# Slopes folded into Q, small work moved off GpSimd, and tables recorded beside the MLPs in a three-block transformer kernel

## The chip, the cores and the metric

One core of a Trainium2 chip runs the whole program. The metric is the device time of one execution in microseconds (us). TensorE, VectorE (DVE in the rows), ScalarE (ACT), GpSimd (POOL) and SyncE (SP, which issues the DMAs) each run their own instructions in order and wait for each other by semaphores.

## The reference, cut to what matters

The input is one sequence of 512 tokens with 1024 features, in float32. Block 1 is an MLA attention (12 heads, rotary part of 32) with a cross attention on 256 memory rows, then an MLP with squared ReLU. Block 2 has a sliding-window attention (SWA, 12 query heads over 4 key heads, ALiBi slopes and sinks) and again cross attention and MLP. Block 3 has a gated short convolution beside an NSA attention (compressed, selected and windowed keys, 8 heads, rotary part of 64), a gated merge, and an FFN with a width-3 causal convolution.

```python
# SWA: scores, slopes, sinks
sc = jnp.einsum('bnqhgd,bnkhd->bnhgqk', q, kk) * (HEAD_DIM ** -0.5)
dist = (pos_q[..., :, None] - pos_k[..., None, :]).astype(jnp.float32)
sc = sc - slopes[None, None, :, :, None, None] * dist[:, :, None, None]
sc = jnp.where(valid[None, :, None, None], sc, NEG)
p = jax.nn.softmax(jnp.concatenate([sc, sink], axis=-1), axis=-1)[..., :-1]
# second block: rotation by positions_2, y_a = a_b * conv(a_c * a_x)
# FFN: g = causal_dwconv(gu[..., :D_FF_2], w) + b; x + (silu(g) * gu[..., D_FF_2:]) @ w_ffn_out
```

## The kernel before

Everything is kept transposed: features on the 128 partitions, the 512 tokens along the free axis, so that the state is eight tiles `x` of 128x512. Float32 products are made of rounded parts: each weight chunk of 128x512 is loaded (`raw`), rounded by ScalarE (`h`), and the rest is taken by a subtraction (`l`); activations are split in the same way. `dense` then does three matmuls for each block of 128 features: h by h, h by l, l by h, into a PSUM bank (`psd`), and an eviction function follows. `fetch_chunk` does the loading and splitting: the subtraction lies on GpSimd for the chunks whose first key begins with one of `POOL_KEYS` (SWA's Q, the convolution path, MLA's uq and ukv), otherwise on VectorE.

`Norm.tile` squares each feature tile on ScalarE and adds the squares up, on GpSimd unless the caller says VectorE; `Boundary.tile` does so for two norms at once. `normalize` divides softmax rows on GpSimd; `rope` and `proj_group` rotate by a product with `cos` on GpSimd and one with `sin` on VectorE; `conv` makes the first of three taps on GpSimd. In SWA, `scores` makes for each head a bias of the distance table `nd` times eight times the slope, on GpSimd, which the masking instruction in `soft` adds to the scores. `rope_tables` makes sine and cosine of 512 positions with 11 instructions on VectorE and two Sin activations on ScalarE.

The program is first recorded (`Trace.add`, with the instructions that each depends on) and then ordered by a planner, `Trace.schedule`. It simulates the five engines with the costs of `_op_cost`. Whenever an engine is free, it takes the ready instruction of the highest priority, which is the recording order (`later` shifts it). An instruction whose page or PSUM bank can't be had yet is parked (the test below); an instruction of a much later part may start early if it is ready and the pages claimed up to its own part leave room for its page. What this gives is the order in which each engine runs the program. Weight loads are shifted forward by 80 instructions.

```python
            for t in o.tiles:
                if t.slot is None:
                    k = t.key
                    if not free[k] or (t.first > cur and load[k][cur:t.first].max() >= cap[k]):
                        return k
```

Tiles: `pgf` and `pgr` are the page pools (20 of float32, 50 of rounded float32), `sm` small columns, `psd`, `pss`, `pst`, `pso` PSUM banks (dense, scores, transposes, outputs), `cstt` the constants, `vecs` the gains. All recorded instructions have one line, L414, so rows are told apart by tiles.

Of the kernel before, what the change touches and what calls it, by code (L numbers as in the profile page):

```python
# [11 lines left out]
FT = mybir.dt.float32  # L12
# [5 lines left out]
P = 128  # L18
# [9 lines left out]
AHEAD = 80  # L28
POOL_KEYS = ("swa_q", "n_a", "uq", "ukv")
NFR = 50  # L30
# [151 lines left out]

NCST = 648


def pack_const():
    c = np.zeros((P, NCST), np.float32)
    i = np.arange(P)
    c[i, i] = 1.0
    c[i ^ 16, 128 + i] = 1.0  # L190
    c[:, 256:384] = np.where(i[None, :] <= i[:, None], 0.0, BIG)
    rel = 128 + i[:, None] - np.arange(256)[None, :]
    c[:, 384:640] = np.where((rel >= 0) & (rel < 128), 0.0, BIG)
    inv32 = (10000.0 ** (-(np.arange(16) * 2.0) / 32)).astype(np.float32)
    inv64 = (10000.0 ** (-np.arange(32) / 32.0)).astype(np.float32)
# [5 lines left out]
    c[:, 645] = i >= 64  # L201
    return c

# [146 lines left out]
class Trace:  # L350
    def __init__(self, nc):
        self.real_nc = nc
        self.ops = []
        self.bias = 0
        for name in ENGINES:
            setattr(self, name, Recorder(self, name))

    @contextmanager
    def later(self, n):
        self.bias += n  # L360
        yield
        self.bias -= n

    def add(self, name, method, args, kw):
# [31 lines left out]
        for v in writes:  # L396
            t, b = v.tile, v.box()
            t.writes = [w for w in t.writes if not (b[0] <= w[1][0] and b[1] >= w[1][1] and b[2] <= w[1][2] and b[3] >= w[1][3])]
            t.reads = [w for w in t.reads if w[0] == o.i or not (b[0] <= w[1][0] and b[1] >= w[1][1] and b[2] <= w[1][2] and b[3] >= w[1][3])]
            t.writes.append((o.i, b))  # L400
        o.preds = preds
        out_costs = writes if writes else [v for v in reads]
# [132 lines left out]
class Norm:  # L535
    def __init__(self, net, src, gains, d, name, into=None, adder="gpsimd"):
        self.into, self.adder = into, getattr(net.nc, adder)
        self.net, self.src, self.gains, self.d, self.name = net, src, gains, d, name
        self.n = src[0].shape[-1]
        self.h = [None] * len(src)  # L540
        self.l = [None] * len(src)
        self.acc = None
# [24 lines left out]
class Boundary:  # L567
# [9 lines left out]
    def tile(self, m):  # L577
# [3 lines left out]
        for j in range(2):  # L581
# [4 lines left out]
            else:  # L586
                q = net.pg("bq")
                nc.scalar.activation(q, x, AF.Square, **kw)
                nc.gpsimd.tensor_tensor(self.acc[j], self.acc[j], q, op=OP.add)

# [22 lines left out]
class Net:  # L613
    def __init__(self, ctx, tc, aps):
# [9 lines left out]
        self.wtiles = {}  # L624
        self.first_key = {}
        for key, j, _, _ in self.plan:
            self.first_key.setdefault(self.blocks[key, j][0], key)

# [24 lines left out]
    def fetch_chunk(self, i):  # L653
# [7 lines left out]
        nc.scalar.copy(h[:, :n], raw[:, :n])  # L661
        eng = nc.gpsimd if self.pool_chunk(i) else nc.vector
        eng.tensor_tensor(l[:, :n], raw[:, :n], h[:, :n].bitcast(FT), op=OP.subtract)
        self.wtiles[i] = (h, l)

    def pool_chunk(self, i):
        return self.first_key[i].startswith(POOL_KEYS)

# [302 lines left out]
    def mla(self, nx, osh, osl):  # L971
# [67 lines left out]
        def proj_group(g):  # L1039
            def rev(p):  # L1040
# [4 lines left out]
                nc.vector.tensor_tensor(w, r, sin, op=OP.mult)  # L1045
                nc.gpsimd.tensor_tensor(u, u, cos, op=OP.mult)
                nc.vector.tensor_tensor(u, u, w, op=OP.add)
# [8 lines left out]
        def proj_pair(p):  # L1056
# [8 lines left out]
            def kev(ps):  # L1065
                for j in range(2):
                    h = 2 * p + j
                    K[h] = self.pg("K")
                    nc.scalar.copy(K[h][0:64], ps[64 * j:64 * j + 64])
                    nc.gpsimd.tensor_scalar(K[h][64:96], kr[64:96], 1.0, 1.0, op0=OP.mult, op1=OP.mult)  # L1070
            self.dense([(f"uq_n{p}", P, qev)], ch[:3], cl[:3])
# [27 lines left out]
        for p in range(6):  # L1099
# [8 lines left out]
            os_set(p, out)  # L1108

    def swa(self, nx, osh, osl):  # L1110
        nc = self.nc
# [45 lines left out]
        nc.vector.tensor_scalar(nsink, self.vec("sinks", 0, 12), -1.0, None, op0=OP.mult)  # L1157

# [8 lines left out]
        def proj_pair(p):  # L1167
            def ev(ps):
                u = self.pg("sq")
                nc.vector.tensor_tensor(u, ps, nx.R, op=OP.mult)  # L1170
                Q[2 * p], Q[2 * p + 1] = self.qstack(u, "sqs")
            self.dense([(f"swa_q{p}", P, ev)], nx.h, nx.l)

        def scores(h):
            k1, k2 = kk[h // 3]
            slope8 = 8.0 * float(np.float32(2.0 ** (-8.0 * (h + 1.0) / 12.0)))
            bias = [self.pg("sb") for _ in range(2)]
            B = [bias[b // 2][:, (b % 2) * 256:(b % 2) * 256 + 256] for b in range(4)]
            nc.gpsimd.tensor_scalar(bias[0][:, 128:], nd[0][:, 128:], slope8, 1.0, op0=OP.mult, op1=OP.mult)
            nc.gpsimd.tensor_scalar(bias[1], nd[1], slope8, 1.0, op0=OP.mult, op1=OP.mult)  # L1180
            nm, sm = self.sm("nm"), self.sm("sum")
# [3 lines left out]
            for b in range(4):  # L1185
# [4 lines left out]
                self.mm(p[:, :n], Q[h][:, b * P:b * P + P], k2[:, k0:k0 + n], False, True)  # L1190
                self.soft(p[:, :n], n, B[b][:, 256 - n:], 0.125, nsink[:, h:h + 1], nm[:, b:b + 1], sm[:, b:b + 1], dst[b])
            e = self.sm("se")
# [37 lines left out]

    def mlp(self, i, nx, after):
        nc = self.nc
# [17 lines left out]
        first = True  # L1250
        for kind, b in MLP_ORDER:
            if kind == "up":
# [7 lines left out]
    def first_block(self, stop):  # L1260
        for i in range(2):
# [9 lines left out]
            if i == 0:  # L1271
                self.mlp(i, n2, nx.tile)
                nx.finish()
            elif stop == "mlp1":
                self.mlp(i, n2, lambda m: None)
            else:
                b = Boundary(self)
                self.mlp(i, n2, b.tile)
                b.finish()
                return b  # L1280
            if stop == f"mlp{i}":
                return

    def second_block(self, nx, stop):
# [12 lines left out]
        nc.sync.dma_start(sel, self.a["sel"])  # L1297
        posr = self.pg("posr2", I32)
        pr = self.a["posr2"]
        nc.sync.dma_start(posr, bass.AP(tensor=pr.tensor, offset=pr.offset, ap=[[0, P], [1, S]]))  # L1300
        cos, sin = self.rope_tables(posr, self.cst[:, 642:643], self.cst[:, 643:644], "r64")
        blk2 = self.cst[:, 644:646]
# [185 lines left out]
        def a_path(m):  # L1488
# [218 lines left out]
```

## Time and profile before

| | |
|---|---|
| runs shown, median (lowest, highest) | 1887.12 us (1885.49, 1887.37) |
| profiled execution, its own time | 1889.12 us |
| its span in the profile | 1887.3 us |
| TensorE matmul busy | 1848.9 us, 98% |
| VectorE busy | 1163.5 us, 62% |
| ScalarE busy | 836.9 us, 44% |
| GpSimd busy | 354.3 us, 19% |
| mean granted clock of TensorE | 0.995 |

The span reaches from the first to the last instruction of the profiled execution, whose own time lies a little outside it. The stages, by the slices of the page: MLA and cross attention to 215 us, output product and first MLP to 600, SWA to 737, output product and second MLP to 1098, the boundary and NSA to 1350, the merge to 1530, the FFN to the end.

### The profile page before, as it was taken

How to read it: one execution, taken by the hardware profiler on the slowest of the kernel's cores; microseconds unless marked ns; L12 is line 12 of the kernel's file. 1: busy time of each engine (PE TensorE's matmuls, PEld its weight loads, DVE VectorE, ACT ScalarE, POOL GpSimd, SP SyncE). 2: the span in 40 equal slices, each digit the busy share in tenths (PEclk: the TensorE clock that was granted, in tenths of full speed). 3: DMA queues.
4: the chain of work that ended last, by engine and by line, in shares of the span. 5: the costliest groups of instructions: out<-in, count | busy, mean ns of one | idle time of the engine just before them, and what ended most of it. 6: DMA issues, size and time to landing. Idle time of an engine off the chain costs nothing.

```text
span 1887.3 us, 25092 instructions
## 1 busy us (share of the span) xinstructions
PE 1848.9 (98%) x8749; PEld 1522.6 (81%) x8749; DVE 1163.5 (62%) x2293; ACT 836.9 (44%) x1674; POOL 354.3 (19%) x406
## 2 busy tenths in 40 slices
PE   7999999999999998999999999999999999999998
PEld 6877788888888876888888887778888888888887
DVE  8977954444546688544434367777755567774752
ACT  7688544242324676442324245457533333332321
POOL 1263300000001553000000041555200122110100
PEclk9999999999999999999999999899999999999999
DMA  5412233333333221333333323211133333333332
GB/s 188 125 42 61 67 102 99 95 98 98 95 95 90 69 56 45 98 98 96 98 98 95 98 63 101 76 51 40 58 99 98 98 89 99 98 98 97 95 100 72
DMA packets 92151, 166.99 MB, mean 88 GB/s; under 512 B 10612, under 2 KB 12408, under 8 KB 92024
## 3 DMA queue, kind: packets, MB, share of 16 engines
q1 hardware_dynamic: 92024, 165.40, 30.3%
q8 instruction: 68, 1.11, 0.2%
q14 instruction: 59, 0.48, 0.1%
HBM read 161.68 MB, written 2.10 MB: 87 GB/s over the span
## 4 chain that ended last, share of the span: by engine, by line
PE 89%; DVE 7%; ACT 2%; issue 1%; DMA 1%; POOL 0%; SPq 0%; DVEq 0%; ACTq 0%; POOLq 0%
PE psd L414 79%; PE pst L414 4%; PE pss L414 3%; DVE pgf L414 3%; PE pso L414 3%; DVE pgr L414 2%; DVE l L414 1%; DVE sm L414 1%; ACT pgf L414 1%; ACT pgr L414 0%; DMA raw<-w 0%; DVE x L414 0%; POOL pgf L414 0%; SPq L414 0%; ACT h L414 0%
## 5 line engine op out<-in xcount | busy, mean ns | idle before, releaser
L414 PE MATMUL psd<-pgr,h 128*128 128x512 f32 (+1 forms) x4590 | 1435.2, 392 | 13.1 <-ACT pgr L414 12.0
L414 PEld LDWEIGHTS psd<-pgr,h 128*128 128x128 f32 x4590 | 858.7, 188 | 191.5 <-ACT pgr L414 13.1
L414 PE MATMUL psd<-pgr,l 128*128 128x512 f32 (+1 forms) x2295 | 897.0, 391 | 0.0
L414 DVE TENSOR_TENSOR l<-raw,h 128x512 fp32r<-128x512 f32 (+1 forms) x551 | 430.1, 783 | 457.1 <-ACT h L414 455.0
L414 ACT CAST h<-raw 128x512 fp32r<-128x512 f32 (+2 forms) x601 | 369.2, 616 | 696.9 <-PE psd L414 602.5
L414 PEld LDWEIGHTS psd<-pgr,l 128*128 128x128 f32 x2295 | 432.3, 188 | 88.3 <-issue 1.9
L414 POOL TENSOR_TENSOR pgf<-pgf,pgf 128x512 f32<-128x512 f32 (+1 forms) x96 | 128.5, 1342 | 1058.4 <-ACT pgf L414 769.9
L414 DVE TENSOR_TENSOR pgr<-pgf,pgr 128x512 fp32r<-128x512 f32 (+4 forms) x184 | 127.4, 694 | 12.5 <-ACT pgr L414 7.4
L414 ACT CAST pgr<-pgf 128x512 fp32r<-128x512 f32 (+4 forms) x184 | 108.2, 590 | 54.0 <-POOL pgf L414 31.0
L414 ACT ACTIVATE pgf<-pgf 128x512 f32<-128x512 f32 (+2 forms) x125 | 74.8, 602 | 110.6 <-DVE pgf L414 110.5
L414 DVE TENSOR_TENSOR pgf<-psd,pgf 128x512 f32<-128x512 f32 (+2 forms) x100 | 65.5, 657 | 57.5 <-PE psd L414 55.9
L414 PE MATMUL pso<-pgr,pgr 128*128 128x512 f32 (+3 forms) x368 | 90.0, 340 | 5.3 <-DVE pgf L414 2.9
L414 DVE TENSOR_TENSOR pgr<-pst,pgr 128x512 fp32r<-128x512 f32 (+1 forms) x126 | 73.8, 610 | 14.3 <-ACT pgr L414 14.1
L414 POOL TENSOR_TENSOR l<-raw,h 128x512 fp32r<-128x512 f32 (+1 forms) x50 | 67.4, 1357 | 75.4 <-ACT h L414 43.7
L414 POOL TENSOR_SCALAR pgf<-pgf,sm 128x256 f32<-128x256 f32 (+3 forms) x128 | 69.2, 558 | 62.7 <-DVE sm L414 46.3
L414 PE MATMUL pst<-cstt,pgf 128*128 128x128 f32 x436 | 75.4, 277 | 2.5 <-POOL pgf L414 1.1
L414 DVE CUSTOM_DVE_ANT_0 pgf<-pss,cmask 128x256 f32<-128x256 f32 (+3 forms) x144 | 65.4, 470 | 17.6 <-PE pss L414 16.2
L414 ACT CAST pgr<-pst 128x512 fp32r<-128x512 f32 (+1 forms) x126 | 62.8, 529 | 27.0 <-PE pst L414 25.9
L414 PEld LDWEIGHTS pso<-pgr,pgr 128*128 128x128 f32 x368 | 58.4, 189 | 19.6 <-ACT pgr L414 7.2
L414 PE MATMUL pss<-pgr,pgr 128*128 128x256 f32 (+4 forms) x320 | 68.6, 309 | 3.9 <-DVE sm L414 3.5
L414 ACT ACTIVATE pgf<-pgf,sm 128x256 f32<-128x256 f32 (+3 forms) x128 | 65.8, 516 | 14.1 <-DVE sm L414 13.7
L414 PEld LDWEIGHTS pst<-cstt,pgf 128*128 128x128 f32 x436 | 52.1, 140 | 19.2 <-POOL pgf L414 6.3
(119 smaller groups left out, 1137.0 us busy)
## 6 DMA issues: line engine op xcount, KB each, us to landing
raw<-w SPq DMA_DIRECT2D x588, 256.0 KB, 2.6
x<-xT SPq DMA_DIRECT2D x8, 256.0 KB, 5.5
out<-x SPq DMA_DIRECT2D x8, 256.0 KB, 2.0
pgf<-pgf SPq DMA_DIRECT2D x24, 64.0 KB, 2.0
pgf<-aux SPq DMA_DIRECT2D x5, 256.0 KB, 2.7
pgf<-memT SPq DMA_DIRECT2D x4, 256.0 KB, 5.4
raw<-w SPq DMA_DIRECT2D x7, 140.0 KB, 2.1
raw<-w SPq DMA_DIRECT2D x4, 192.0 KB, 2.7
```

The source lines that it names most:

```text
L414: getattr(getattr(nc, names[o.eng]), o.method)(*[r(x) for x in o.args], **{k: r(v) for k, v in o.kw.items()})
```

## The change

`POOL_KEYS` goes: all weight splits are on VectorE. The norm and boundary adds, the rotary products with `cos`, the copies of the rotary key into `K`, and the two page products of the convolution path move from GpSimd to VectorE. The first tap of `conv` moves from GpSimd to ScalarE. GpSimd keeps `normalize`, NSA's gating, the merge sum and the FFN's gate product. In SWA, Q is divided by eight times the slope when it is evicted (six new constant columns), the distance table is added as it stands, and the scale in `soft` becomes 0.125 times that number; the 24 bias instructions go. The distance tables of SWA and the 64-wide rotation tables of the second block are recorded in the first and the second MLP, after its first two steps; for the latter the position load (`hold`) depends on the last instruction recorded before it.

```diff
+    @contextmanager
+    def hold(self):
+        self.held = len(self.ops) - 1
+        yield
+        self.held = None
...
+        if self.held is not None:
+            preds.add(self.held)
...
-    def __init__(self, net, src, gains, d, name, into=None, adder="gpsimd"):
+    def __init__(self, net, src, gains, d, name, into=None, adder="vector"):
...
-                nc.gpsimd.tensor_tensor(self.acc[j], self.acc[j], q, op=OP.add)
+                nc.vector.tensor_tensor(self.acc[j], self.acc[j], q, op=OP.add)
...
-        eng = nc.gpsimd if self.pool_chunk(i) else nc.vector
-        eng.tensor_tensor(l[:, :n], raw[:, :n], h[:, :n].bitcast(FT), op=OP.subtract)
+        nc.vector.tensor_tensor(l[:, :n], raw[:, :n], h[:, :n].bitcast(FT), op=OP.subtract)
...
-                nc.gpsimd.tensor_tensor(u, u, cos, op=OP.mult)
+                nc.vector.tensor_tensor(u, u, cos, op=OP.mult)
...
-                    nc.gpsimd.tensor_scalar(K[h][64:96], kr[64:96], 1.0, 1.0, op0=OP.mult, op1=OP.mult)
+                    nc.vector.tensor_copy(K[h][64:96], kr[64:96])
...
+    def swa_positions(self):
...
+        self.swa_tables = ND, nsink
...
-                nc.vector.tensor_tensor(u, ps, nx.R, op=OP.mult)
+                nc.vector.scalar_tensor_tensor(u, ps, self.cst[:, 646 + p:647 + p], nx.R, op0=OP.mult, op1=OP.mult)
...
-            nc.gpsimd.tensor_scalar(bias[0][:, 128:], nd[0][:, 128:], slope8, 1.0, op0=OP.mult, op1=OP.mult)
-            nc.gpsimd.tensor_scalar(bias[1], nd[1], slope8, 1.0, op0=OP.mult, op1=OP.mult)
...
-                self.soft(p[:, :n], n, B[b][:, 256 - n:], 0.125, nsink[:, h:h + 1], nm[:, b:b + 1], sm[:, b:b + 1], dst[b])
+                self.soft(p[:, :n], n, ND[b][:, 256 - n:], float(0.125 * SLOPE8[h]), nsink[:, h:h + 1], nm[:, b:b + 1], sm[:, b:b + 1], dst[b])
...
-        for kind, b in MLP_ORDER:
+        for step, (kind, b) in enumerate(MLP_ORDER):
+            if step == 2:
+                aside()
...
+    def nsa_tables(self):
+        nc = self.nc
+        posr = self.pg("posr2", I32)
+        pr = self.a["posr2"]
+        with nc.hold():
+            nc.sync.dma_start(posr, bass.AP(tensor=pr.tensor, offset=pr.offset, ap=[[0, P], [1, S]]))
+        self.rope64 = self.rope_tables(posr, self.cst[:, 642:643], self.cst[:, 643:644], "r64")
...
-            nc.gpsimd.tensor_tensor(u, u, cos, op=OP.mult)
+            v.tensor_tensor(u, u, cos, op=OP.mult)
...
-                nc.gpsimd.tensor_tensor(t, t, nx.R, op=OP.mult)
+                v.tensor_tensor(t, t, nx.R, op=OP.mult)
...
-                nc.gpsimd.tensor_tensor(u, u, st["y"], op=OP.mult)
+                v.tensor_tensor(u, u, st["y"], op=OP.mult)
...
-            nc.gpsimd.tensor_scalar(y, t, w[2], 1.0, op0=OP.mult, op1=OP.mult)
+            nc.scalar.activation(y, t, AF.Copy, scale=w[2])
...
-            nc.gpsimd.tensor_scalar(y, t, w[2], b, op0=OP.mult, op1=OP.add)
+            nc.scalar.activation(y, t, AF.Identity, scale=w[2], bias=b)
```

## Rows read from the trace of the kernel before

**Rows 1.** Table by stage: length, busy time (instructions) of each engine, granted clock, DMA.

```profile
50.00:200.00 150.00, 148.23 (x841) 118.99 (x842) 124.32 (x354) 118.71 (x288) 62.31 (x86) 1.00 0.26 73
...
640.00:705.00 65.00, 62.76 (x351) 50.18 (x349) 55.30 (x144) 49.86 (x135) 34.60 (x55) 1.00 0.18 50
705.00:737.00 32.00, 25.20 (x156) 20.39 (x155) 28.34 (x80) 24.93 (x68) 13.72 (x26) 1.00 0.07 17
737.00:1098.00 361.00, 361.00 (x1595) 298.37 (x1595) 173.67 (x266) 133.67 (x227) 16.95 (x12) 1.00 0.34 97
1098.00:1150.00 52.00, 51.12 (x253) 42.00 (x252) 35.38 (x93) 20.50 (x37) 13.54 (x10) 1.00 0.24 67
1170.00:1206.00 36.00, 30.89 (x172) 25.71 (x171) 26.35 (x42) 16.76 (x30) 18.02 (x12) 0.86 0.41 117
1206.00:1350.00 144.00, 141.06 (x760) 116.11 (x761) 115.04 (x364) 88.80 (x222) 75.30 (x92) 0.99 0.17 48
1530.00:1883.00 353.00, 352.56 (x1554) 291.33 (x1552) 214.22 (x283) 102.95 (x169) 48.22 (x44) 1.00 0.33 95
```

**Rows 2.** Chain that ended last, 700 to 738 us: start, us, what.

```profile
728.53 1.28 ACT L414
729.82 1.16 ACT pgf L414 x2
```

**Rows 3.** Instructions on page tiles, VectorE, 714 to 732 us: duration ns min/median/max, starts.

```profile
L414 DVE TENSOR_SCALAR pgf<-pgf x4: 415/428/589, 717.9 to 731.7; 128x512 f32<-128x512 f32 x4
...
L414 DVE SCALAR_TENSOR_TENSOR pgf<-pgf,pgf x3: 677/687/693, 721.6 to 725.4; 128x512 f32<-128x512 f32 x3
...
L414 DVE TENSOR_SCALAR pgf<-pgf,cstt x2: 488/508/528, 716.7 to 730.5; 128x512 f32<-128x512 f32 x2
L414 DVE CAST pgf<-pgf x1: 422/422/422, 714.8 to 714.8; 128x512 f32<-128x512 int32 x1
L414 DVE TENSOR_TENSOR pgf<-pgf x1: 691/691/691, 731.0 to 731.0; 128x512 f32<-128x512 f32 x1
```

**Rows 4.** Waits of TensorE, 1150 to 1206 us: total us, times, longest.

```profile
PE pso L414 <- ACT pgf L414: 5.1, 2, 3.0
```

**Rows 5.** VectorE in order of time, 1174 to 1188 us: start, us, instruction.

```profile
1182.17 3.36 DVE L414 TENSOR_TENSOR pgf<-pgf,pgf 128x512 f32<-128x512 f32 x2
```

**Rows 6.** GpSimd in order of time, the same stretch.

```profile
1181.55 1.74 POOL L414 TENSOR_TENSOR pgf<-pgf,pgf 128x512 f32<-128x512 f32 x1
1183.26 3.40 POOL L414 TENSOR_TENSOR l<-raw,h 128x512 fp32r<-128x512 f32 x2
```

**Rows 7.** VectorE groups, 260 to 545 us, no GpSimd: busy us, mean ns | idle before.

```profile
L414 DVE TENSOR_TENSOR l<-raw,h 128x512 fp32r<-128x512 f32 x106 | 73.3, 692 | 139.5 <-ACT h L414 139.3
```

**Rows 8.** VectorE in order of time, 741 to 750 us, GpSimd silent beside this row.

```profile
745.12 1.28 DVE L414 TENSOR_TENSOR l<-raw,h 128x512 fp32r<-128x512 f32 x2
```

**Rows 9.** GpSimd groups, 50 to 215 us (first attention), as rows 7.

```profile
L414 POOL TENSOR_TENSOR l<-raw,h 128x512 fp32r<-128x512 f32 x11 | 15.0, 1375 | 8.3 <-ACT h L414 5.9 <-ACT pgr L414 1.4 <-POOL l L414 1.0
...
L414 POOL TENSOR_SCALAR pgf<-pgf 32x512 f32<-32x512 f32 x12 | 9.1, 762 | 42.9 <-DVE pgf L414 38.3 <-PE pst L414 2.8 <-DVE pgr L414 1.1
...
L414 POOL TENSOR_TENSOR pgf<-pgf,pgf 128x512 f32<-128x512 f32 x3 | 3.9, 1286 | 7.0 <-PE pst L414 7.0
```

**Rows 10.** GpSimd groups, 640 to 737 us (SWA), as rows 7.

```profile
L414 POOL TENSOR_TENSOR l<-raw,h 128x512 fp32r<-128x512 f32 x4 | 5.7, 1431 | 0.2
```

**Rows 11.** GpSimd groups, 1150 to 1350 us (NSA), as rows 7.

```profile
L414 POOL TENSOR_TENSOR l<-raw,h 128x512 fp32r<-128x512 f32 x24 | 33.5, 1401 | 31.1 <-ACT h L414 31.0
L414 POOL TENSOR_TENSOR pgf<-pgf,pgf 128x512 f32<-128x512 f32 x14 | 19.4, 1383 | 57.1 <-DVE l L414 39.0 <-DVE pgf L414 7.9 <-PE pso L414 6.8
```

**Rows 12.** VectorE in order of time, from 199 us (tail of the first attention).

```profile
201.78 0.87 DVE L414 CAST pgf<-pgf 128x512 f32<-128x512 int32 x1
```

**Rows 13.** VectorE groups, 50 to 215 us, as rows 7.

```profile
L414 DVE TENSOR_TENSOR l<-raw,h 128x512 fp32r<-128x512 f32 x24 | 17.8, 756 | 0.4 <-ACT h L414 0.2
...
L414 DVE COPY pgf<-pgf 32x512 f32<-32x512 f32 x12 | 6.9, 574 | 0.3
```

More of the change, by code (lines that the diff above doesn't have):

```diff
@@ L28 @@
 AHEAD = 80
-POOL_KEYS = ("swa_q", "n_a", "uq", "ukv")
 NFR = 50
@@ L180, in pack_vec @@
     return np.ascontiguousarray(np.concatenate(parts, axis=1))
-NCST = 648
+NCST = 656
+SLOPE8 = np.float32(8.0) * (2.0 ** (-8.0 * (np.arange(12) + 1.0) / 12.0)).astype(np.float32)
 def pack_const():
@@ L201, in pack_const @@
     c[:, 645] = i >= 64
+    for p in range(6):
+        c[:, 646 + p] = np.where(i < 64, 1.0 / SLOPE8[2 * p], 1.0 / SLOPE8[2 * p + 1])
     return c
@@ L362, in later @@
         self.bias -= n
+    @contextmanager
+    def hold(self):
+        self.held = len(self.ops) - 1
+        yield
+        self.held = None
     def add(self, name, method, args, kw):
@@ L624, in __init__ @@
         self.wtiles = {}
-        self.first_key = {}
-        for key, j, _, _ in self.plan:
-            self.first_key.setdefault(self.blocks[key, j][0], key)
     def nm(self, s):
@@ L661, in fetch_chunk @@
         nc.scalar.copy(h[:, :n], raw[:, :n])
-        eng = nc.gpsimd if self.pool_chunk(i) else nc.vector
-        eng.tensor_tensor(l[:, :n], raw[:, :n], h[:, :n].bitcast(FT), op=OP.subtract)
+        nc.vector.tensor_tensor(l[:, :n], raw[:, :n], h[:, :n].bitcast(FT), op=OP.subtract)
         self.wtiles[i] = (h, l)
-    def pool_chunk(self, i):
-        return self.first_key[i].startswith(POOL_KEYS)
     def W(self, key, k):
@@ L1108, in mla @@
             os_set(p, out)
-    def swa(self, nx, osh, osl):
+    def swa_positions(self):
         nc = self.nc
-        kk = []
-        def kev(p):
-            u = self.pg("sk")
-            nc.vector.tensor_tensor(u, p, nx.R, op=OP.mult)
-            k1 = [self.pg("kk1", FR) for _ in range(2)]
-            k2 = [self.pg("kk2", FR) for _ in range(2)]
-            self.kstack(u, k1, k2)
-            kk.extend(zip(k1, k2))
-        vv = []
-        def vev(t, p):
-            vv.append(self.vsplit(p, 4, nx.RT[:, t:t + 1], "sv"))
-        qs = []
-        def xev(p):
-            u = self.pg("qx")
-            nc.vector.tensor_tensor(u, p, nx.R, op=OP.mult)
-            qs.extend(self.qstack(u, "qxs"))
-        self.dense([(f"swa_k{m}", P, kev) for m in range(2)], nx.h, nx.l, il=2)
-        self.dense_tm("swa_v", 256, nx.h, nx.l, 4, vev)
         lo_r, hi_r = self.pg("plr"), self.pg("phr")
@@ L1157, in swa, with kev, vev, xev @@
         nc.vector.tensor_scalar(nsink, self.vec("sinks", 0, 12), -1.0, None, op0=OP.mult)
+        self.swa_tables = ND, nsink
+    def swa(self, nx, osh, osl):
+        nc = self.nc
+        kk = []
+        def kev(p):
+            u = self.pg("sk")
+            nc.vector.tensor_tensor(u, p, nx.R, op=OP.mult)
+            k1 = [self.pg("kk1", FR) for _ in range(2)]
+            k2 = [self.pg("kk2", FR) for _ in range(2)]
+            self.kstack(u, k1, k2)
+            kk.extend(zip(k1, k2))
+        vv = []
+        def vev(t, p):
+            vv.append(self.vsplit(p, 4, nx.RT[:, t:t + 1], "sv"))
+        qs = []
+        def xev(p):
+            u = self.pg("qx")
+            nc.vector.tensor_tensor(u, p, nx.R, op=OP.mult)
+            qs.extend(self.qstack(u, "qxs"))
+        self.dense([(f"swa_k{m}", P, kev) for m in range(2)], nx.h, nx.l, il=2)
+        self.dense_tm("swa_v", 256, nx.h, nx.l, 4, vev)
+        ND, nsink = self.swa_tables
         self.dense([(f"swa_x{m}", P, xev) for m in range(2)], nx.h, nx.l)
@@ L1175, in scores @@
             k1, k2 = kk[h // 3]
-            slope8 = 8.0 * float(np.float32(2.0 ** (-8.0 * (h + 1.0) / 12.0)))
-            bias = [self.pg("sb") for _ in range(2)]
-            B = [bias[b // 2][:, (b % 2) * 256:(b % 2) * 256 + 256] for b in range(4)]
-            nc.gpsimd.tensor_scalar(bias[0][:, 128:], nd[0][:, 128:], slope8, 1.0, op0=OP.mult, op1=OP.mult)
-            nc.gpsimd.tensor_scalar(bias[1], nd[1], slope8, 1.0, op0=OP.mult, op1=OP.mult)
             nm, sm = self.sm("nm"), self.sm("sum")
@@ L1229, in wo, with mlp @@
         nxt.finish()
-    def mlp(self, i, nx, after):
+    def mlp(self, i, nx, after, aside):
         nc = self.nc
@@ L1271, in first_block @@
             if i == 0:
-                self.mlp(i, n2, nx.tile)
+                self.mlp(i, n2, nx.tile, self.swa_positions)
                 nx.finish()
             elif stop == "mlp1":
-                self.mlp(i, n2, lambda m: None)
+                self.mlp(i, n2, lambda m: None, self.nsa_tables)
             else:
                 b = Boundary(self)
-                self.mlp(i, n2, b.tile)
+                self.mlp(i, n2, b.tile, self.nsa_tables)
                 b.finish()
@@ L1282, in first_block @@
                 return
+    def nsa_tables(self):
+        nc = self.nc
+        posr = self.pg("posr2", I32)
[3 more added lines that the diff above has]
+        self.rope64 = self.rope_tables(posr, self.cst[:, 642:643], self.cst[:, 643:644], "r64")
     def second_block(self, nx, stop):
@@ L1297, in second_block @@
         nc.sync.dma_start(sel, self.a["sel"])
[L1298 to L1301, printed above, removed]
+        cos, sin = self.rope64
         blk2 = self.cst[:, 644:646]
```

## The prediction

> **What bounds the kernel now.** I read the page's busy times by slice first and cut the span into stages by them, then a table of busy time by stage, then the chain that ended last and the waits of TensorE in the stages that are not full. TensorE is busy nearly always, so only the places where it stands, or runs at less than its pace, can pay. The stage table shows where they are [rows 1]: in both MLPs and the FFN it is busy from end to end (361.00 of 361.00 us in the second MLP, 352.56 of 353.00 in the FFN), and there no other engine's saving can count. The first attention (50 to 200 us) loses 1.8 us. The SWA stage loses 2.2 us up to 705 and then 6.8 us in its last 32. The boundary (1098 to 1150) loses 0.9, the NSA stretch from 1170 to 1206 loses 5.1 and runs at a mean granted clock of 0.86, and the rest of NSA loses 2.9.
>
> Two places need a closer look. At the end of SWA the chain is VectorE from 706 to 727 us almost without a break, followed by a ScalarE table load and two Sin activations [rows 2]. VectorE is busy 28.34 of 32 us there [rows 1]. Eleven of its instructions are not SWA work at all: they are the 64-wide rotation tables of the second block, which have no early input and which the planner took as filler [rows 3]. In NSA the 5.1 us are one wait in two pieces, TensorE for the squares on ScalarE [rows 4]. Going back: ScalarE stood at the head of its queue for VectorE, which took 3.36 us over two instructions [rows 5], beside a GpSimd rope product of 1.74 us and two splits of 3.40 us together [rows 6].
>
> **What a moved instruction costs.** With GpSimd silent, a 128x512 two-input instruction on VectorE spans 0.69 us [rows 7], and two in a row take 1.28 [rows 8], so one more costs about 0.60. On GpSimd a split takes 1.38 to 1.43 us and a product 1.29 to 1.38 [rows 9 to 11]. In the pair of [rows 5] VectorE lost 3.36 - 1.28 = 2.1 us in 3.36 us beside GpSimd, 0.62 us for each us of overlap. So moving one such instruction changes VectorE's work by +0.60 if the two never overlapped and by 0.60 - 1.40 x 0.62 = -0.27 if they always did.
>
> **The change, part by part.**
>
> *Rotation tables into the second MLP.* Leaving the SWA tail: VectorE 0.42 + 3 x 0.69 + 2 x 0.51 + 4 x 0.43 + 0.69 = 5.9 us [rows 3], ScalarE 1.28 + 1.16 = 2.4 [rows 2], together 8.3 us of the chain. This part will really move: its DMA is tied to the last instruction recorded before it, and everything else hangs on that DMA. What remains late is the last head's own chain (transposes, copy, add, split), which I can't shorten. Bounds 0 to 8.3; since TensorE stands 6.8 us there and some 2 of those belong to the last head, I take **-5**. In the MLP the same instructions lie beside TensorE at 361 of 361, with VectorE at 174 and ScalarE at 134 [rows 1]: cost nothing. The held DMA does stop SyncE's queue, and weight loads stand behind it; they run ahead by the eight h/l chunk buffers, each 12 matmuls, and the instruction it waits for is in the stream that paces those loads anyway. If that cover were gone, one load's wait would fall on TensorE once.
>
> *SWA position tables.* These are recorded in the first MLP, but without a tie. Their inputs exist since the start, and the planner starts whatever is ready when an engine is free and pages allow. They already run long before SWA: the first big one starts at 201.8 us, in the tail of the first attention [rows 12], and the others follow within 14 us. Recording them earlier doesn't hold them back. I expect them to stay there: **0**. If they did leave, the tail there would give about 4 us (some ten instructions of 0.3 to 0.9 us in its last fifteen).
>
> *Slopes into Q.* 24 GpSimd instructions go; the eviction of Q gains a pointer scalar. TensorE hardly waits on them, so directly nothing; the four swa_q splits after 640 us (4 x 0.60 = 2.4 us) go onto VectorE, against the contention of those splits' 5.7 us on GpSimd [rows 10] and of the bias tables. Bounds -2 to +2.4, taken **0**; the other swa_q splits come before 640, beside a full TensorE.
>
> *First attention.* Onto VectorE come 11 splits, 3 of three quarters the width, 3 products and 12 K copies [rows 9]: 11 x 0.60 + 3 x 0.47 + 3 x 0.60 + 12 x 0.57 (the like copy of Q in [rows 13]) = 16.7 us. Off GpSimd go 15.0 + 9.1 + 3.9 + 3 x 0.75 x 1.38 = 31.1 us; given back between 0 and 31.1 x 0.62 = 19. VectorE's own splits here average 0.756 against 0.691 undisturbed [rows 7, 13], which is near the lower end, so I take 5: net +12. VectorE goes from 124 to about 136 of 150 us. At 85% busy (640 to 705) TensorE lost 3.4%, here at 83% 1.2% [rows 1]; two more per cent of 150 is **+3**. Bounds 0 and +12 (all of it on the path). The Trainium skill speaks against the copies: GPSIMD Engine Reference, Engine selection, sends two-input work to VectorE but calls one-input work on GpSimd roughly line-rate. The trace agrees only in part (0.76 on GpSimd, 0.57 on VectorE, both with contention); by the rule the 6.9 us of copies should have stayed, and this term would be nearer +1 than +3.
>
> *NSA.* The rope product becomes 0.60 instead of 1.38 to 1.74, no longer waits behind GpSimd's splits, and the VectorE instructions around it lose their stretch. For the product and the two splits of [rows 6] VectorE takes 3 x 0.60 = 1.8 us and gets the 2.1 back. The chain loses the GpSimd steps: of 5.1 us of waits I take **-4** (0 to -5.1). The granted clock was at half after these waits and the small matmuls that follow: 0.14 x 36 = 5.0 us lost at 1.2 in place of 2.4 GHz. The small matmuls stay, so I take half, **-2.5** (0 to -5.0). The Trainium skill (TensorE: Matmul & The Clock Gate, HAM oscillation) describes waits between matmul groups as what makes each group start cold. By that alone all 5.0 would return and the sum would be 2.5 lower. From 1206 to 1350, 17 splits and 8 products (15 us) come onto a VectorE at 115 of 144 us, against up to 21 back: **0** (-2 to +6).
>
> *Boundary and norms.* The adds go from about 1.4 to 0.60 us; two end the boundary's chain, 1.6 us, where TensorE waits 0.9 in all: **-0.5** (0 to -0.9). In the MLPs the same shortening lies under a full TensorE: 0.
>
> *Conv taps on ScalarE.* 4 in NSA, 22 in the FFN, where ScalarE is at 103 of 353 us and TensorE full: 0. No row here shows Identity; if each tap forced a table load there and back, 22 x 2 x 1.28 = 56 us would still fit in ScalarE's idle time.
>
> Sum: -5 - 4 - 2.5 - 0.5 + 3 = **-9**. From the profiled execution's span, 1887.3, that gives 1878.3; its own time, 1889.1, becomes 1880.1. The median of the runs shown, 1887.1, lies at the span, so I predict **1878 us**.
>
> **Rivals.** (1) *Everything comes back:* the SWA tail gives 8.3, NSA 5.1 and 5.0, the boundary 0.9, the rest of NSA 2, and VectorE absorbs the first attention: -21, **1866**. For it: VectorE is the chain at both places. Against: a second chain usually stands close behind. (2) *Given back:* half of the gains, and VectorE's extra 12 us in the first attention costs 5: **1886**, no change. For it: VectorE at 91% there. (3) *Slower:* a split now waits at the head of VectorE's in-order queue for ScalarE's copy or the weight DMA, with evictions and softmax behind it, and TensorE waits for those. GpSimd stood 8.3 us before its splits in the first attention [rows 9] and 31.1 in NSA [rows 11]. With half of both on the path it costs 19 more than forecast: 1878 + 19 = **1897**. It decides from 9 us on, where it eats the gain. Against it: VectorE's 24 own splits in the first attention waited 0.4 us [rows 13]. (4) *The position tables do leave* the first attention: 4 more, part of case 1. That they stay is the part of the change that doesn't do what it says.
>
> **Chances.** 0.2% (3.8 us) is about what a measurement of this kernel can tell from no change. Forecast 0.50 (its own range 1872 to 1883), case 1 0.20, case 2 0.17, case 3 0.13. Faster 0.70, same 0.17, slower 0.13. The range must hold most of cases 1 and 2 and leaves out the ends of the bounds (-27 and +20): **1862 to 1891**.
>
> **What would show it.** Right: no Sin table load and none of the eleven table instructions between 700 and 737, but in the second MLP, and less than 3 us of TensorE idle in the last 30 us of SWA; no wait of TensorE over 1 us for ScalarE's squares in NSA; a granted clock above 0.92 there; two-input VectorE instructions back at 0.69 us. The position tables still near 200 us. Wrong: waits of VectorE for ScalarE's h above 5 us in the first attention or in NSA, TensorE idle above 6 us between 50 and 200, or clock dips that stay though the waits are gone.

## The result, and the profile after

The changed kernel takes **1859.4 us** (median; 1858.6 to 1860.0) against 1886.7 for the kernel before in the same comparison: ratio 0.9856, 95% interval 0.9839 to 0.9873. That is 27.3 us faster where 9 were forecast; the time lies below the range, and the direction is as forecast. The profiled execution took 1858.63 us.

First the page's busy times after, and the table by stage of both kernels, cut at the first and the last addition of an output into `x`, so that both have the same matmuls between the same borders (first attention, first MLP, SWA, second MLP, NSA with the merge, and not shown the rest). The columns are those of [rows 1]. After:

```profile
PE 1836.0 (99%) x8749; PEld 1517.8 (82%) x8749; DVE 1175.4 (63%) x2421; ACT 856.3 (46%) x1700; POOL 166.9 (9%) x228
```

```profile
0.00:211.38 211.38, 199.41 (x1074) 160.16 (x1075) 188.97 (x522) 159.56 (x365) 38.97 (x70) 1.00 0.32 98
211.38:589.97 378.59, 378.59 (x1673) 313.21 (x1672) 191.24 (x310) 141.15 (x242) 0.00 (x0) 1.00 0.33 98
589.97:722.14 132.17, 129.72 (x771) 109.93 (x770) 109.41 (x299) 97.22 (x255) 37.13 (x64) 1.00 0.20 57
722.14:1100.45 378.31, 378.31 (x1671) 312.76 (x1670) 194.80 (x308) 145.44 (x246) 0.00 (x0) 1.00 0.33 97
1100.45:1463.83 363.38, 360.51 (x1845) 299.90 (x1844) 253.60 (x647) 177.13 (x375) 60.90 (x72) 1.00 0.26 77
```

The same borders in the kernel before:

```profile
0.00:216.20 216.20, 201.57 (x1076) 161.21 (x1077) 181.22 (x484) 159.27 (x365) 76.55 (x110) 0.99 0.32 97
...
594.50:737.97 143.47, 134.42 (x771) 110.97 (x770) 111.56 (x297) 100.49 (x258) 64.39 (x97) 1.00 0.19 54
737.97:1117.04 379.07, 379.07 (x1675) 313.47 (x1674) 186.85 (x278) 143.04 (x243) 27.79 (x19) 1.00 0.33 97
1117.04:1493.15 376.11, 366.08 (x1842) 302.29 (x1841) 250.10 (x608) 173.62 (x371) 109.75 (x116) 0.98 0.26 74
```

The stages are those of the two profiled executions. The one of the kernel before lies 2 us above its median, so their spans differ by 30.5 us and not 27.3. Of these 30.5 us the first attention gives 4.8, SWA 11.3, NSA 12.7 and the rest 1.7. Two things are to be seen. VectorE's work hardly grew (1163.5 to 1175.4 us) though GpSimd's fell from 354.3 to 166.9. And SWA's gain is only in part TensorE standing still (9.0 to 2.5 us): the same 771 matmuls also took 134.4 us of "busy" before and 129.7 after, both at full clock. Matmuls in a row overlap: in the rows below, from 30 to 36 us of the changed kernel, one counts 0.39 us of busy time and two in a row 0.62 together. The more matmuls stand apart, the more busy time the same number shows, so a thin stream looks full.

```profile
29.64 0.39 PE L426 MATMUL psd<-pgr,h 128*128 128x512 f32 x1
30.10 0.62 PE L426 MATMUL psd<-pgr,h 128*128 128x512 f32 x2
```

The waits of TensorE in SWA (590 to 738 us) and where [rows 4] had 5.1 us (1150 to 1206 us), after:

```profile
PE pst L426 <- POOL pgf L426: 2.1, 7, 0.6
PE psd L426 <- ACT pgr L426: 0.2, 1, 0.2
...
PE pso L426 <- ACT pgf L426: 0.7, 1, 0.7
PE psd L426 <- DVE l L426: 0.4, 1, 0.4
```

VectorE in order of time there, which answers to [rows 5, 6]; and its groups in NSA (1150 to 1335 us), with its waits for ScalarE's `h`:

```profile
1162.91 1.29 DVE L426 TENSOR_TENSOR pgf<-pgf,pgf 128x512 f32<-128x512 f32 x2 [0.21 <-DMA pgf<-pgf]
1164.12 0.68 DVE L426 TENSOR_TENSOR l<-raw,h 128x512 fp32r<-128x512 f32 x1
1164.73 0.68 DVE L426 TENSOR_TENSOR pgf<-pgf,pgf 128x512 f32<-128x512 f32 x1
```

```profile
L426 DVE TENSOR_TENSOR l<-raw,h 128x512 fp32r<-128x512 f32 x43 | 29.1, 688 | 3.3 <-ACT h L426 3.3
L426 DVE TENSOR_TENSOR pgf<-pgf,pgf 128x512 f32<-128x512 f32 x21 | 14.4, 699 | 1.6 <-DMA pgf<-pgf 1.5
```

The pair of 3.36 us is 1.29, two-input instructions are back at 0.69 to 0.70 us, and 43 splits wait 3.3 us in all for `h`, where GpSimd's 24 waited 31.1 [rows 11] before.

The tables in VectorE's and ScalarE's order: the SWA position tables still lie in the tail of the first attention, the 64-wide tables moved into the second MLP:

```profile
195.98 0.42 DVE L426 CAST pgf<-pgf 128x512 f32<-128x512 int32 x1
...
845.55 0.43 DVE L426 CAST pgf<-pgf 128x512 f32<-128x512 int32 x1
```

```profile
851.99 1.28 ACT L426 ACT_TABLE_LOAD   x1
```

### The profile page after: what moved, and what is told of

It reads as the page before. It is cut to its first block, busy times and chain, and to the rows that moved or that the text cites. A ratio compares the mean times of both kernels' runs of the same rounds, so it can differ in the third digit from the quotient of the medians.

```text
span 1856.8 us, 24974 instructions
## 1 busy us (share of the span) xinstructions
PE 1836.0 (99%) x8749; PEld 1517.8 (82%) x8749; DVE 1175.4 (63%) x2421; ACT 856.3 (46%) x1700; POOL 166.9 (9%) x228
## 4 chain that ended last, share of the span: by engine, by line
PE 89%; issue 6%; DVE 2%; POOL 1%; DMA 1%; SPq 0%; ACT 0%; POOLq 0%; DVEq 0%; ACTq 0%
PE psd L426 80%; PE pst L426 3%; PE pso L426 3%; PE pss L426 3%; POOL pgf L426 1%; DVE pgf L426 1%; DVE pgr L426 1%; SPq L426 0%; DMA cstt<-cst 0%; DMA raw<-w 0%; DVE l L426 0%; ACT pgf L426 0%; DVE sm L426 0%; DMA pgf<-pgf 0%; ACT L426 0%
## 5 line engine op out<-in xcount | busy, mean ns | idle before, releaser
L426 DVE TENSOR_TENSOR l<-raw,h 128x512 fp32r<-128x512 f32 (+2 forms) x601 | 434.3, 726 | 448.0 <-ACT h L426 446.3
L426 POOL TENSOR_SCALAR pgf<-pgf,sm 128x256 f32<-128x256 f32 (+3 forms) x128 | 74.8, 601 | 626.8 <-DVE sm L426 570.0
L426 DVE TENSOR_TENSOR pgr<-pgf,pgr 128x512 fp32r<-128x512 f32 (+4 forms) x184 | 121.6, 662 | 9.1 <-ACT pgr L426 3.8
L426 POOL TENSOR_SCALAR pgf<-pgf,sm,gates 128x128 f32<-128x128 f32 (+1 forms) x64 | 50.6, 803 | 549.6 <-PE psd L426 478.6
L426 DVE TENSOR_TENSOR pgf<-psd,pgf 128x512 f32<-128x512 f32 (+2 forms) x94 | 61.3, 655 | 46.6 <-PE psd L426 46.0
L426 POOL TENSOR_TENSOR pgf<-pgf,pgf 128x512 f32<-128x512 f32 x30 | 40.2, 1340 | 423.9 <-DVE pgf L426 423.9
L426 DVE TENSOR_TENSOR x<-psd,x 128x512 f32<-128x512 f32 x80 | 55.2, 691 | 25.0 <-PE psd L426 24.9
```

What stands on the lines that cost most here:

```text
L426: getattr(getattr(nc, names[o.eng]), o.method)(*[r(x) for x in o.args], **{k: r(v) for k, v in o.kw.items()})
```

## The experiments

Stage lengths in us, cut as above; "idle" is TensorE's in that stage, "half" the time at 1.2 GHz in NSA. Each ratio is to runs of the kernel before in the same comparison.

| kernel | median | ratio (95%) | first att. | SWA (idle) | NSA (idle, half) |
|---|---|---|---|---|---|
| before | 1886.7 | | 216.2 | 143.5 (9.0) | 376.1 (10.0, 13.7) |
| tables alone | 1885.4 | 0.9991 (0.9982 to 1.0000) | 214.8 | 143.5 (8.7) | 376.0 (10.2, 13.7) |
| slopes alone | 1883.1 | 0.9975 (0.9965 to 0.9985) | 214.1 | 135.8 (5.2) | 373.9 (6.3, 17.1) |
| engine moves alone | 1876.3 | 0.9940 (0.9928 to 0.9952) | 212.7 | 146.5 (10.7) | 364.3 (2.7, 6.8) |
| splits alone | 1889.6 | 1.0006 (0.9997 to 1.0014) | 216.9 | 146.9 (11.1) | 372.4 (5.9, 17.1) |
| other moves alone | 1880.9 | 0.9960 (0.9948 to 0.9973) | 214.9 | 143.6 (8.2) | 371.9 (4.7, 13.7) |
| slopes and tables | 1876.3 | 0.9935 (0.9922 to 0.9947) | 213.2 | 134.6 (4.4) | 374.3 (7.7, 13.7) |
| the same, pages claimed | 1883.1 | 0.9970 (0.9959 to 0.9980) | 213.4 | 140.9 (6.3) | 376.3 (10.1, 13.7) |
| the same, small tiles | 1876.3 | 0.9938 (0.9925 to 0.9952) | 212.9 | 134.3 (3.7) | 376.2 (9.6, 13.7) |
| tables, 2 more pages | 1883.5 | 0.9977 (0.9967 to 0.9986) | 212.2 | 142.3 (6.6) | 376.2 (9.8, 13.7) |
| tables, 5 pages freed | 1882.3 | 0.9970 (0.9958 to 0.9982) | 213.7 | 140.0 (6.4) | 375.2 (8.3, 13.7) |
| after, no slopes | 1875.3 | 0.9937 (0.9925 to 0.9949) | 213.7 | 146.4 (10.0) | 364.1 (2.5, 6.8) |
| after, no tables | 1858.6 | 0.9851 (0.9839 to 0.9864) | 211.0 | 133.4 (3.1) | 366.1 (2.3, 10.2) |
| after, pages claimed | 1872.1 | 0.9916 (0.9902 to 0.9931) | 210.9 | 144.8 (8.5) | 363.3 (3.0, 3.4) |
| after, small tiles | 1859.2 | 0.9858 (0.9839 to 0.9876) | 210.8 | 131.8 (3.0) | 363.8 (3.3, 3.4) |
| after, SWA tables tied | 1857.9 | 0.9839 (0.9825 to 0.9852) | 208.8 | 132.1 (2.5) | 366.1 (2.6, 10.2) |
| after, both ties | 1860.5 | 0.9856 (0.9843 to 0.9869) | 211.3 | 132.0 (2.5) | 364.0 (2.4, 6.8) |
| after, again | 1858.7 | 0.9848 (0.9835 to 0.9861) | 211.5 | 132.2 (2.5) | 363.3 (3.0, 3.4) |

**The three parts alone.** A control that only changes how far weight loads are shifted forward (76 for 80) measured 0.9998 (0.9989 to 1.0006): this other order by itself is worth nothing in the time. Its stages differ from the kernel before by up to 2 us (first attention 214.1, SWA 143.9, NSA 375.2), so a stage's difference of 1 or 2 us says little.

> A control: the kernel before with weight loads recorded 76 instead of 80 instructions ahead, which changes nothing but the planner's order. If the order alone moves the time, this differs by 4 us or more either way and gains of that size in the other runs are not to be read as mechanisms; if not, it stays within 3 us.

Tables alone, with the bias as before:

```diff
+            if step == 2:
+                aside()
```

> The kernel before with the tables alone recorded in the MLPs (the rotation tables tied, the SWA tables not). Theory 1, the SWA tail was held up by the rotation tables: the eleven instructions and the Sin load leave 700 to 737 us, SWA gets 5 to 8 us shorter, all else stays, total -5 to -8 us. Theory 2, the gain comes from GpSimd's work going: under 2 us here. The SWA tables stay near 200 us in either.

A miss. The eleven instructions and the Sin load left the last 32 us of SWA, and VectorE there fell from 28.34 us [rows 1] to this (703.6 to 735.6 us, same distance from the stage's end):

```profile
703.60:735.60 32.00, 27.62 (x167) 22.57 (x167) 25.07 (x71) 23.06 (x64) 11.95 (x22) 1.00 0.06 17
```

but SWA kept its 143.47 us to the hundredth. TensorE's idle time in these 32 us fell from 6.8 us to 4.4, but as much came back earlier in the stage (8.7 in all, for 9.0). The instructions were filler beside the chain that paces the heads. TensorE still waits for the last head:

```profile
PE psd L424 <- ACT pgr L424: 2.5, 2, 2.0
```

Slopes alone:

```diff
-                nc.vector.tensor_tensor(u, ps, nx.R, op=OP.mult)
+                nc.vector.scalar_tensor_tensor(u, ps, self.cst[:, 646 + p:647 + p], nx.R, op0=OP.mult, op1=OP.mult)
...
-            nc.gpsimd.tensor_scalar(bias[1], nd[1], slope8, 1.0, op0=OP.mult, op1=OP.mult)
```

> The kernel before with the slopes folded into Q alone: 24 GpSimd instructions and 24 pages fewer in SWA. Theory 1 (TensorE hardly waits for the bias): 0, within 2 us. Rival, the freed pages and GpSimd time let SWA's heads run closer: SWA 3 to 6 us shorter. The rotation tables may move with the freed pages.

SWA gets 7.7 us shorter, and 7.2 of them are lost again in the output product behind the first attention (first MLP stage 385.5 for 378.3). There the untied 64-wide tables now start at 227.6 us, beside GpSimd's norm additions. VectorE in order of time, and TensorE's wait (215 to 260 us):

```profile
230.88 1.35 DVE L417 SCALAR_TENSOR_TENSOR sm<-pgf,pgf,sm 128x64 f32<-128x64 f32 x1
...
237.36 1.78 DVE L417 SCALAR_TENSOR_TENSOR pgf<-pgf,pgf 128x512 f32<-128x512 f32 x1
```

```profile
PE psd L417 <- DVE x L417: 3.5, 2, 2.9
```

Each of these two stands exactly beside a GpSimd addition of 1.30 us; undisturbed they take 0.27 and 0.68 there. VectorE falls behind with `x`, TensorE waits 3.5 us, and its clock is at half for 6.8 us.

All moves between engines alone (`eng` becomes VectorE in `fetch_chunk`, `nc.gpsimd` becomes `nc.vector` in the additions, products and copies, taps on ScalarE):

> The kernel before with all moves between engines (splits, adds, products, K copies, conv taps), slopes and tables as before. Theory 1 by stage: first attention -5 (as in the changed kernel, against the forecast +3), NSA -12, SWA under -2, total about -17 to -19 us. Rival, the stages help each other: under -10 alone. VectorE's busy time per stage stays within 4% of before because what it takes over equals the stretch that it loses.

11 us, nearly all of it in NSA; SWA gets worse by 3.0. The 17 to 19 us of the expectation did not come.

**The two halves of the moves.** The splits alone, then all the other moves alone:

```diff
-        eng = nc.gpsimd if self.pool_chunk(i) else nc.vector
-        eng.tensor_tensor(l[:, :n], raw[:, :n], h[:, :n].bitcast(FT), op=OP.subtract)
+        nc.vector.tensor_tensor(l[:, :n], raw[:, :n], h[:, :n].bitcast(FT), op=OP.subtract)
```

> The kernel before with the weight splits alone on VectorE. Of the 11.8 us by which all engine moves shortened NSA: theory 1, the splits block GpSimd's queue before the rope product and stretch VectorE, so they carry most: NSA -6 to -9 us, first attention 0 to -2, SWA +1 to +3, total -4 to -8. Rival, the rope and page products' own latency carries it: NSA under -3 here. Rival 3 of the prediction, splits at the head of VectorE's queue hold up other work: NSA or the first attention longer.

> The kernel before with adds, products, K copies and conv taps moved, the weight splits left where they were. All moves gave NSA -11.8 us and SWA +3.0, the splits alone -3.7 and +3.4. Theory 1, the rope product on GpSimd is a link of NSA's chain and waits there behind the splits: NSA -6 to -9 here, SWA within 1 us, first attention -2 to -4, total -9 to -13. Rival, only both together free the chain: NSA under -4.

NSA needs both: 3.7 and 4.2 us alone, 11.8 together, and the time at half clock falls only when both are moved. Each half gave less in NSA than expected of it (6 to 9 us). GpSimd is silent from 1150 to 1195 us only with both moved (6.4 us of work there with the splits alone moved, 9.7 with the others alone, none with both). The splits' 3.4 us in SWA cancel what they give in NSA.

**What the slopes do.** First slopes and tables together; then the same with the two bias pages of each head claimed again by small copies (four of one column), and a control with the same copies into small columns:

```diff
+            bias = [self.pg("sb") for _ in range(2)]
+            for u in bias:
+                nc.gpsimd.tensor_scalar(u[:, :1], nd[0][:, 255:256], 1.0, 1.0, op0=OP.mult, op1=OP.mult)
...
+            for u in bias:
+                nc.gpsimd.tensor_scalar(u[:, 1:2], sm[:, 3:4], 1.0, 1.0, op0=OP.mult, op1=OP.mult)
```

> The kernel before with slopes folded and tables moved, no move between engines. Slopes alone made SWA 7.7 us shorter but the rotation tables, free to start earlier, landed in the output product after the first attention and cost 7.2 us there. Theory 1, the tie of the tables' load saves just that: SWA 133 to 136 us, the first MLP stage back at 378.3, total -9 to -11 us. Rival, the rotation tables were SWA's hold-up after all and slopes only moved them: SWA 136 or more and nothing beyond -4.

> Slopes folded and tables moved, but each head still claims two pages that nothing needs, from its start to the end of its softmax (four one-column GpSimd copies in place of the two wide bias instructions). Theory A, pages: SWA back at 141 to 144 us. Theory B, GpSimd's time: SWA as with slopes and tables, 133 to 136 us, at most 1.5 us longer.

> The control to the run with claimed pages (SWA 140.9 us): the same four one-column GpSimd copies for each head, but into small column tiles, so that no page is claimed. If pages were what made SWA longer there, SWA is 134 to 136 us here, as with slopes and tables; if the copies themselves (their place in GpSimd's queue) did it, 139 to 141.

The claim alone puts back 6.6 us (140.9 against 134.3) where slopes beside tables had taken 8.9 (143.5 to 134.6): most of it is the pages. With the bias kept, two more float pages (and two fewer rounded ones), or the five pages of constants held back until the second MLP, give less:

```diff
-NFR = 50
-NFT = 20
+NFR = 48
+NFT = 22
```

> Tables moved, bias kept on GpSimd, and two pages shifted from the rounded pool to the float32 pool (22 and 48 in place of 20 and 50). Theory A, slopes help because the bias tables of two heads take four pages and the planner can't start the next heads: SWA 3 to 7 us shorter than with tables alone (143.5). Theory B, it is GpSimd's time on the bias (some 17 us of its queue in SWA, and VectorE's stretch beside it): SWA within 1.5 us of 143.5.

> Tables moved, bias kept on GpSimd, and the five page loads of the second block's small weights tied to the second MLP as the position load is; before, they are issued between 165 and 190 us and hold five of the 20 float32 pages through SWA. Theory A, pages: SWA 4 to 8 us shorter than the 143.5 with tables alone, although all of GpSimd's bias work is still there. Theory B, GpSimd's time: SWA 142 to 144. The tail of the first attention may get 1 to 3 us shorter in either, since the sums made from these loads leave it too.

Both miss what the page theory said. Two more pages give 1.2 us of SWA (142.3 for 143.5), where 3 to 7 were expected; taken alone this run would have spoken for GpSimd's time. The five freed pages give 3.5 (140.0), where 4 to 8 were expected.

**Parts taken out of the whole.** Slopes with tables make -12 us and the moves -11, the whole -28. So the changed kernel without the slopes, without the tables, and again itself beside them:

> The changed kernel with the slopes taken out again: the 24 bias instructions stand on GpSimd with their pages, everything else as in the changed kernel. Additive theory: the slopes are worth what they gave with the tables alone, 9 to 10 us in SWA, so SWA is 141 to 142 us and the time 1868 to 1870 us. Synergy theory (the weight splits on VectorE are affordable in SWA only when the bias pages and the bias work are gone, since with splits or all engine moves but no slopes SWA took 146.5 to 146.9): SWA 145 to 148 us, the time 1873 to 1876 us, and NSA stays at 363 to 365 us, since nothing there hangs on the slopes.

> The changed kernel with both tables recorded where they stood in the kernel before, without the tie. Theory A (the tie matters only because slopes folded into Q free pages, so that the 64-wide tables start early): their cast lies near 220 to 260 us in the output product behind the first attention, TensorE loses 3 to 7 us there, and the time is 1862 to 1867 us. Theory B (the tie is worth nothing with VectorE relieved of GpSimd's stretch): 1858 to 1861 us, with the output product and first MLP within 0.5 us of 378.6.

> The changed kernel itself, beside the three others on one chip, so that differences of a few us can be told: 1858.5 to 1860.5 us by every theory.

The parts help each other: on top of the moves the slopes are worth 16.6 us (1875.3 to 1858.7), 14.2 of them in SWA. The tables are worth nothing here either: without the tie they start at 226.2 us as in the slopes-alone run, but with GpSimd silent every instruction keeps its 0.69 us, `x` is on time, and the first MLP stage is 378.6. VectorE in order of time there:

```profile
235.31 0.69 DVE L417 SCALAR_TENSOR_TENSOR pgf<-pgf,pgf 128x512 f32<-128x512 f32 x1
235.91 0.75 DVE L417 SCALAR_TENSOR_TENSOR pgr<-x,vecs,pgr 128x512 fp32r<-128x512 f32 x1
236.57 0.69 DVE L417 TENSOR_TENSOR pgf<-pgf,pgf 128x512 f32<-128x512 f32 x1
```

Then the claim and its control on top of the changed kernel (the diff above, with `ND[0]` for `nd[0]`):

> The changed kernel, in which each SWA head again claims the two bias pages until its sums are done, but only four one-column copies on GpSimd stand in for the bias work. Page theory (most of what the slopes are worth in the whole change, 14 us of SWA, is the pages): SWA 140 to 144 us in place of 132.2, the time 1867 to 1871 us. Work theory (it is the GpSimd bias tables and the stretch they give VectorE): SWA 132 to 135 us, the time 1859 to 1862 us.

> The control to the one before: the same small copies, but into small columns, so that no page is claimed. Both theories: SWA 132 to 134 us, 1859 to 1861 us; if it is as slow as the run with claimed pages, the small copies themselves cost and that run says nothing of pages.

The claim costs 12.9 us (1872.1 against 1859.2), all of it in SWA (144.8 against 131.8). All runs fall in line: the nine with the bias pages free have an SWA of 131.8 to 135.8 us, the ten with these pages claimed, by the bias or by the copies, and the control of the order have 140.0 to 146.9. The 65 us from 45.5 us after the stage's start, claimed, then control, then the changed kernel:

```profile
635.00:700.00 65.00, 60.96 (x340) 48.85 (x338) 54.57 (x150) 49.88 (x137) 26.25 (x68) 1.00 0.16 46
```

```profile
635.00:700.00 65.00, 64.41 (x399) 55.31 (x397) 62.86 (x186) 58.91 (x168) 28.41 (x69) 1.00 0.14 38
```

```profile
635.50:700.50 65.00, 62.74 (x383) 52.24 (x381) 60.28 (x175) 55.98 (x157) 25.73 (x44) 1.00 0.15 42
```

Beside 351 matmuls in the kernel before [rows 1]. The instructions on `pss` alone in the same 65 us (TensorE, its weight loads, VectorE): the kernel before, claimed, control, changed kernel:

```profile
640.00:705.00 65.00, 15.26 (x73) 11.58 (x73) 14.72 (x36) 1.00 0.18 50
635.00:700.00 65.00, 14.21 (x72) 12.04 (x72) 15.95 (x38) 1.00 0.16 46
635.00:700.00 65.00, 19.85 (x98) 15.68 (x98) 20.26 (x49) 1.00 0.14 38
635.50:700.50 65.00, 15.75 (x86) 13.05 (x86) 18.43 (x44) 1.00 0.15 42
```

With four float pages to a head 36 and 38 score blocks pass VectorE's masking, with two 49 and 44. Fewer heads are under way at once: counted over these 65 us in the traces, the score blocks that VectorE has masked and GpSimd has not yet normalised are 3.4 on average in the kernel before, 3.5 with the claim, 5.0 in the control and 4.7 in the changed kernel. TensorE gets fewer matmuls in between.

**More on top of the change.** The SWA position tables tied into the first MLP (`with nc.hold():` around their first loop), and that with the five loads of constants tied into the second MLP:

> The changed kernel with SWA's position tables tied to the first MLP in the same way, so that they really leave the tail of the first attention. Rival 4 of the prediction: 4 us there, total 1.5 to 4 us below the changed kernel (0.9835 to 0.985 of before). Rival: like the rotation tables in SWA they sit beside the chain, not on it: within 1 us of the changed kernel.

> The changed kernel, plus two ties in the manner of the 64-wide tables: the SWA position tables wait for the last instruction recorded before them in the first MLP, and the five loads of second-block constants go into the second MLP. Theory A (the tail of the first attention and the pages of SWA were set by this early filler): the first attention stays at the 208.8 us that it had with the first tie alone (211.4 changed kernel), and SWA, rid of five claimed pages, loses another 1 to 3 us of 132.1: 1853 to 1856 us. Theory B (with the bias pages gone the pages no longer bind in SWA): SWA stays within 0.5 us, and the time is that of the first tie alone, 1857.5 +- 1.5.

Neither differs from the changed kernel beyond the intervals (0.9839 and 0.9856 against its 0.9856 and 0.9848). Five more free pages change nothing in SWA (132.0), so pages no longer bind there. The first attention of 208.8 us did not return in the second run, so what the tie is worth there stays open.

## Why the prediction was wrong, step by step

**The step that failed first: slopes into Q, "TensorE hardly waits on them, so directly nothing", 0 with bounds -2 and +2.4.** Measured: SWA 8.9 us shorter beside the tables, and the time 16.6 us shorter on top of the moves. I priced the 24 instructions by who waits for them and not by what they hold. Their tiles were two of a head's four float pages, and the planner holds a head back until it has its pages; no wait in the trace names that. What TensorE waits for GpSimd in the whole of SWA (590 to 738 us, before) bears out "hardly waits":

```profile
PE pst L414 <- POOL pgf L414: 0.8, 3, 0.4
```

12.9 of the 16.6 us are shown to be the claim. No run takes apart the other 3.7, which are a difference of runs and can hold the work of the bias instructions. What the trace did show was SWA at 351 matmuls in 65 us with TensorE 97% busy [rows 1]: I took the 97% as full.

Without this step the forecast would have looked good by luck: the changed kernel without the slopes takes 1875.3 us, 12 less than before where 9 were forecast, but the tables give nothing of their 5, SWA is 2.9 longer, the first attention is shorter and not longer, and NSA gives 12.

**Rotation tables, -5:** measured 0, alone and in the whole. They moved where I said, and of "what remains late is the last head's own chain" all remained. Instructions without an early input stood in the list of the chain because the engine was free for them, not because the chain needed that time. The tie guards against the 7 us of the slopes-alone run, but only while GpSimd adds beside it.

**SWA position tables, 0:** right; they stayed near 200 us.

**First attention, +3:** the stage got 4.8 us shorter (2.7 to 3.4 against the 214.8 and 214.1 us of the tables and the slopes alone, which leave its code as it was). Where I looked the term was right in sign: from 50 us to the tail TensorE's idle time went from 1.8 us [rows 1] to 3.4 (145.00 - 141.57 in the row below), with VectorE at 90% (forecast 91). But I had left out 30 to 50 us. There TensorE waited 2.6 us for VectorE, whose small instructions on `sm` had taken about 0.70 us each beside the memory norm's additions on GpSimd (25.8 to 32.6 us) and take 0.15 after; the mean granted clock was 0.91. One of them and the stretch, before, then both after:

```profile
28.73 0.70 DVE L414 TENSOR_TENSOR sm<-sm 128x4 f32<-128x4 f32 x1
30.00:50.00 20.00, 17.45 (x79) 13.63 (x78) 18.61 (x50) 9.52 (x18) 2.43 (x3) 0.91 0.23 66
```

```profile
26.72 0.15 DVE L426 TENSOR_TENSOR sm<-sm 128x4 f32<-128x4 f32 x1
30.00:50.00 20.00, 20.00 (x98) 16.50 (x97) 19.50 (x85) 10.99 (x20) 0.00 (x0) 1.00 0.20 59
50.00:195.00 145.00, 141.57 (x811) 112.50 (x809) 130.68 (x343) 117.93 (x288) 35.13 (x60) 1.00 0.25 72
```

That is 2.6 + 0.09 x 20 = 4.4 us; the run with the other moves alone has 20.00 of 20.00 there too, the splits alone do not. (The former loses 5.8 us from 50 to 200, and its stage takes 214.9 all the same.) In the tail TensorE's idle time went from 1.9 us to 0.1, which gives 1.8. VectorE's work from 50 us to the tail grew by 6.4 us (124.32 to 130.68) for a forecast 12: over the whole stage its splits went from 727 to 694 ns on average, the 32x512 copies from 574 to 458. By the rule named in the prediction (the Trainium skill, GPSIMD Engine Reference, Engine selection) the copies could have stayed. No run here moves them alone, and 0.46 us on VectorE against 0.76 on GpSimd [rows 9] speaks for the move.

**NSA, -4 and -2.5:** the mechanism was right, and the term of the waits was too small. Idle time fell by 7.2 us (10.0 to 2.9) for a forecast 4, not only in the two waits of [rows 4]. The time at half clock fell from 13.7 to 3.4 us, worth 5.1, the upper bound; but in other runs with the same moves 6.8 to 10.2 us at half clock stay (table), worth 3.5 to 1.7, so the 2.5 lies within what the runs give. By the rule named in the prediction (the Trainium skill, TensorE: Matmul & The Clock Gate, HAM oscillation) all of it returns once the waits are gone. The trace agrees in part: idle time is 2.3 to 3.3 us in all these runs, and 3.4 to 10.2 us at half clock stay.

**Rivals.** "Everything comes back" (1866) named the right places in NSA but not the one in SWA. "Slower", splits at the head of VectorE's queue, is refuted in NSA (3.3 us of waits, longest 1.0). In SWA without the slopes the splits do cost 3 us, but by waits for `h` that is not shown: VectorE waits 5.5 us for it there (after, no slopes) and 4.7 in the changed kernel, which loses nothing.

Of my list of signs, those for NSA (granted clock 0.95 from 1152 to 1188 us), for the 0.69 us and for the tables came true, as did TensorE idle under 3 us at the end of SWA (0.2 us in the last 32), though for another reason than the tables.

**Left open:** why the splits cost 3 us in SWA with the bias and nothing without it. With the pages claimed and no bias work the same cost is there (144.8 us with the moves, 140.9 without), so pages are most of it; how the two meet in the planner is not shown.

## What to carry to other kernels

Ask of an instruction that you remove what buffers it holds and for how long, not only who waits for it; a claim can be put back alone, beside a control, to price it. Judge TensorE's fullness by matmuls per stretch as well as by its busy share. Filler that shows in the chain is not the cause of it until a run without it is shorter. Here, moves off GpSimd were worth most where together they silenced it in a stretch.

## What the runs showed of the hardware

- A VectorE instruction with two SBUF inputs beside a GpSimd one is stretched at each of the three lengths seen: 0.15 to 0.70 us beside a row of additions, 0.27 to 1.35 and 0.68 to 1.78 beside one of 1.30 us. The masking, whose scores come from PSUM, is not: in the kernel before, 16 such instructions of 128x256 (`pgf<-pss,cmask`) that lie wholly beside a two-input GpSimd one took 424 ns in the median, and 420 with GpSimd silent. In NSA the product group went from 1114 to 699 ns.
- The 22 taps on ScalarE in the FFN (Identity, unknown in the prediction) take 814 ns each and brought no table load: five loads in the whole execution before and after.
- The same program differs by 4 us from one execution to the next, and the mean granted clock of TensorE differs with it: the changed kernel without its tables took 1862.1 us at a mean granted clock of 0.997 and 1858.0 to 1858.6 at 0.999.
